# Fewer table transposes, two-tile copies, later stores and a reordered entry in a hybrid decoder block

## The chip, the core and the metric

The kernel runs on one core of one Trainium2 chip. The metric is the device time of an execution in microseconds (us); the time of a kernel is the median of its runs. Engines are called by their short names: PE (TensorE), DVE (VectorE), ACT (ScalarE), POOL (GpSimd) and SP (SyncE, which here only issues DMAs). ACT issues DMAs too, in the same instruction stream as its arithmetic.

## The reference

One decoder layer over 1024 tokens of width 1024, in float32: two SwiGLU feed-forward halves around a merge of two token mixers, with an RMS norm ahead of each part.

```python
def reference(x, ...):                       # x: (1, 1024, 1024)
    h = x + 0.5 * swiglu(rms_norm(h), w1, w3, w2)          # FFN 1, d_ff = 2816
    u = rms_norm(h)
    q, k, v, pz, gate_logits = split(u @ w_in)             # 3 x 768, 512, 2 x 1024 columns
    gates = sigmoid(gate_logits)
    y_attn = dilated_mixture_attention(q, k, v) @ w_branch_attn
    y_pool = multiscale_pool(pz, pool_w, pool_scale) @ w_branch_pool
    h = h + (gates[0] * y_attn + gates[1] * y_pool) @ w_out
    h = h + 0.5 * swiglu(rms_norm(h), w1', w3', w2')       # FFN 2
    return rms_norm(h, final_norm)
```

The attention has 3 groups of 4 heads of 64 dimensions, with windows and dilations (128, 1), (512, 4) and (2048, 16). The first 16 of the 64 dimensions of q and k are rotated by tables of cosines and sines (RoPE). The groups are combined by their softmax denominators.

## The kernel before, in words

**Products.** Every float32 operand is split into a high part, which ACT rounds to the matmul's format, and a low part, the rest, which DVE or POOL subtracts. A product of two operands is three matmuls: high by high, high by low, low by high (`three`). On top of that lies a 2 x 2 block scheme with seven products instead of eight (Strassen in Winograd's form): `Sevens` and `Quad` for the products with stationary weights, `Down` for the down projections. A `Quad` product has 12 matmuls of 128x512 with k-major order, the three terms of one k together; its weight operand (`operand`) is a sum on DVE, a high half on ACT (L304) and a low half on POOL or DVE (L307). Operands are prepared two products ahead.

**Stages, with their times in the profile.** The entry of FFN 1 to 60 us; its up projections to 460; its down projection (`Down.run`, 42 steps of 24 matmuls) to 632; the entry of the mix to 690; the input projection to 1045; attention to 1167; merges and the product with `w_out` to 1262; then FFN 2 in the same three parts, and the final norm to 1916.

**Order.** All of it stands in `tc.manual_schedule()`: every engine runs its instructions in the order in which the program writes them, and waits for the tiles that others write. Moving a call in the source moves its instructions in the queue of each engine that it uses, ahead of or behind whatever the other calls put there.

**What the change touches.**

- `Entry.run` takes the eight tiles of a stage's norm in turn: it scales rows, transposes them on PE into the blocks of X, and keeps high and low halves of the block sums (`Rows` and `Parts`; their `lower` is the DVE subtraction that frees a PSUM bank), with the first products of the stage in between. Its last tile (t = 7) is written out apart.
- `load_rope`, `widen`, `make_table`: the RoPE tables arrive by token. POOL copies them four times over (L1318), PE transposes 24 blocks of 128x128 (L1325), ACT copies the result (L1327) and stores it in DRAM (L1328), one group of heads at a time, as tasks of FFN 1's `Down.run` (steps 9 to 22). `load_table` on SP reads them back later.
- `Mix.rotate` is a generator that the input projection advances by one yield unit a product. For both halves `a` it stores the 16 rotary rows of q or k (L1103, two stores) and the whole rows (L1105, one store) through ACT, then reads the rotary rows back in another order (L1108), also through ACT. The number that it yields is how many products pass before it goes on.
- `Mix.store` stores a block of gates, by SP, and the very last one by ACT (L1094).
- `gather` copies the outputs of one attention slot from PSUM into the group's buffer `own` (L1701), two copies of 64x128 a slot; `values` computes two slots into one bank.
- `merge(k)` multiplies the attention's output by `w_branch_attn` for one block (six matmuls, L1803), times the gate on DVE (L1805), plus the other branch on POOL; `split_o` and `step_o` (L1979, L1991) are the operands and the matmuls with `w_out`.
- `Down.begin` splits the operands of a step: `b`, the weights, then `a`, the left side (L745 on ACT, L749 on DVE or, for some steps' `a`, on POOL).
- `with_gain`, `send_out`, `send_low` close the final norm: squares on ACT (L2171), the gain and scale on DVE (L2167, L2181, L2191) or ACT (L2185), and the output's DMAs.

Of the kernel before, what the change touches and what calls it, by code (L numbers as in the profile page):

```python
# [126 lines left out]
def tile_block(  # L127
# [163 lines left out]
    class Sevens:  # L291


        def __init__(self, name, X, fw, fs=None):
            self.name, self.X, self.fw, self.fs = name, X, fw, fs or fw
            self.n_lo = 0
            self.by_term = False
# [12 lines left out]
        def product(self, p, w, x, start=True):  # L310
            hi, lo = self.X[x]
            order = [(k, q) for k in range(4) for q in range(3)]
            if self.by_term:
                order = [(k, q) for q in (0, 2, 1) for k in range(4)]
            for n, (k, q) in enumerate(order):
                r = slice(k * P, (k + 1) * P)
                a, b = three((w[:, 0, r], w[:, 1, r]), (hi[:, k, :], lo[:, k, :]))[q]
                pe.matmul(p, a, b, start=(start and n == 0), stop=(n == 11), skip_group_check=not start)  # L318
# [66 lines left out]
    class Rows:  # L385


        def __init__(self, X, what, src, t, tag="acc"):
            q = t % 4
            self.hi, self.lo = (v[:, :, q * P:(q + 1) * P] for v in X[what])  # L390
            p = self.flat = bank(tag, f"x_{what}_{t}")
            self.p = p.rearrange("p (k q) -> p k q", k=4)
            for k in range(4):
                pe.transpose(self.p[:, k, :], src[:, k * P:(k + 1) * P], ident)
            ac.activation(self.hi, self.p, AF.Copy)
# [20 lines left out]
    class Entry:  # L416
# [18 lines left out]
        def run(self, high, after, first=0):  # L435
# [84 lines left out]
            after(t)  # L520

# [106 lines left out]
    def up(sv, sums, between, name, room, begun):  # L628
# [3 lines left out]
        with tc.manual_schedule():  # L632
            last = ORDER[-1]
            items = [(q, w, m, out) for q in begun for w, out in ((q.A, q.a_out), (q.B, q.b_out))
                     for m in ORDER if m not in (1, 2)]
            then = Pair(sv, len(begun), sums)
            ahead = [(w, m) for _, w, m, _ in items] + [(then.A, m) for m in ORDER[:2]]
            parts, res = [], []
            for k, (q, w, m, out) in enumerate(items):
                ahead[k + 2][0].operand(ahead[k + 2][1])  # L640
                res.append(w.run(m))
                if m == last:
                    raws.depth = 6 if q is not begun[-1] else 4
                if k > 0:
                    p, _, m, out = items[k - 1]
                    out(m, res[k - 1])
# [58 lines left out]
    class Down:  # L705
# [3 lines left out]
        def __init__(self, name, sums, half_tile, pair):  # L709
# [5 lines left out]
            self.n_lo = 0  # L715
# [17 lines left out]
        def split(self, side, srcs, n):  # L733
# [4 lines left out]
            self.n_lo += 1  # L738
            whole = len(srcs) == 1 and srcs[0].shape[1] > 1
            eng = gp if self.n_lo % 4 == 0 and 1 < n < self.last_shared else ve  # L740
# [27 lines left out]
        def begin(self, i):  # L768
# [3 lines left out]
            w = self.split("b", self.right.pop(i), i)  # L772
# [3 lines left out]
            self.ops[i] = (self.split("a", [self.g.pop(i)], i), w)  # L776
# [99 lines left out]
    def begin_up1():  # L876
# [55 lines left out]
        sv1.by_term = True  # L932
        entry.product(0)
        sv1.by_term = False
# [82 lines left out]
    table_dram = [dram.tile([P, 2, HALF], F32, name=f"table{g}") for g in range(GROUPS)]  # L1017
# [19 lines left out]
    class Mix:  # L1037
# [51 lines left out]
        def store(self):  # L1089
            yield 3  # L1090

            queue = nc.sync if self.q < len(MIX) - 1 else nc.scalar
            for a in range(2):
                queue.dma_start(gate_dram[self.g][:, a], self.y[a])  # L1094

        def rotate(self):
# [4 lines left out]
            for a in range(2):  # L1101
# [4 lines left out]
                yield 1 + 2 * a  # L1106
# [192 lines left out]
    with sbuf("steps1", "right") as pool:  # L1299
# [7 lines left out]
        given, wide = [], {}  # L1307

        def load_rope():
            given.append(own_row("rope")[:, :768].rearrange("p (i c) -> p i c", i=GROUPS * NT))  # L1310
            nc.sync.dma_start(given[0], c_rope)

        def widen(g):
            wide[g] = own_row(f"wide{g}").rearrange("p (s j t a c) -> p s j t a c", s=2, j=4, t=2, a=4)
            for s in range(2):
                for t in range(2):
                    src = given[0][:, g * NT + 4 * t:g * NT + 4 * t + 4, None, 16 * s:16 * s + 16]
                    gp.tensor_copy(wide[g][:, s, :, t], src.to_broadcast([P, 4, 4, 16]))  # L1318

        def make_table(g, tag):  # L1320
            tab = own_row(f"table{g}").rearrange("p (s c) -> p s c", s=2)
            for s in range(2):
                p = bank(tag, f"table{g}_{s}")
                for j in range(4):
                    pe.transpose(p[:, j * P:(j + 1) * P], wide[g][:, s, j].rearrange("p t a c -> p (t a c)"),  # L1325
                                 ident)
                ac.activation(tab[:, s, :], p, AF.Copy)  # L1327
            nc.scalar.dma_start(table_dram[g], tab)  # L1328
# [20 lines left out]
        def scale_in_place(t):  # L1349
# [179 lines left out]
    def by_token(g, d, v):  # L1529
# [6 lines left out]
        return [(by[b], v.rearrange("p (r b) c -> b p r c", b=2)[b]) for b in range(2)]  # L1536
# [69 lines left out]
    def masked(s):  # L1606
# [7 lines left out]
        else:  # L1614
            if i == 0:
                own_stats[hp, g] = att_small.tile([P, NT, 4], F32, name=f"own_stats{hp}_{g}")
            st = own_stats[hp, g][:, i, :]
# [52 lines left out]
    def values(q):  # L1670
        both = bank("acc", f"o{q}")
        for s in (2 * q, 2 * q + 1):
# [12 lines left out]
            d["o"] = p  # L1685
# [3 lines left out]
    own = {}  # L1689

    def gather(s):

        hp, g, i = slots[s]
        p = T.pop(s)["o"]
        t0, step, _ = tokens(g, i)
        cols = slice(t0, t0 + step * (P - 1) + 1, step)
        if i == 0:
            own[hp, g] = sums_o.tile([P, S], F32, tag="o", bufs=HPAIRS * GROUPS, name=f"o{hp}_{g}")
        for a in range(2):
            r = slice(a * HD, (a + 1) * HD)  # L1700
            ve.tensor_copy(own[hp, g][r, cols], p[r, a, :])  # L1701
# [134 lines left out]
    with tc.manual_schedule():  # L1836
        load_branch(1)
        load_ring(uses[1], ring_place(1))
        load_gate(1)
# [4 lines left out]
        for q in range(N // 2):  # L1844
# [13 lines left out]
            if q > 2:  # L1858
                gather(2 * q - 6)
                gather(2 * q - 5)  # L1860
# [30 lines left out]
        gather(2 * q - 6)  # L1891
        gather(2 * q - 5)
# [5 lines left out]
        for s in range(2 * q - 4, 2 * q):  # L1898
            gather(s)
# [123 lines left out]
    with tc.manual_schedule():  # L2023
        for k in range(6):
# [5 lines left out]
            if k > 1:  # L2030
# [4 lines left out]
        for k in range(6, 11):  # L2035
# [121 lines left out]
    def low_half(t):  # L2157
# [4 lines left out]
        if t == 6:  # L2162
# [15 lines left out]
    def send_out(t):  # L2178
# [5 lines left out]
        if t > 5:  # L2184
# [10 lines left out]
    def after2(m, t):  # L2195
# [5 lines left out]
        elif m == len(DOWN) - 1:  # L2201
# [6 lines left out]
            elif t < 3:  # L2208
                send_low(3 + t)
            else:  # L2210
# [98 lines left out]
```

## Time and profile before

| | us |
|---|---|
| median of 3 runs | 1920.96 (1918.78 to 1922.57) |
| the profiled execution | 1918.08 |
| its span in the profile | 1916.3 |

The page gives busy times of the engines over the span. A line of a timeline has the start in us, the duration in us, the engine, the line of the kernel, the operation, what it writes and reads, and the number of instructions drawn together; in brackets stands how long the engine sat idle before it and what released it. ACTq and SPq are the DMA issues in the queues of ACT and SP. The granted TensorE clock of the profiled execution is 0.999 of full speed.

### The profile page before, as it was taken

What the parts mean: (1) busy time and instruction counts of PE and PEld (TensorE: products, weight loads), DVE (VectorE), ACT (ScalarE), POOL (GpSimd) and SP (SyncE); (2) the same over time, 40 slices, a digit from 0 to 9 for tenths busy, and PEclk for the clock granted to TensorE, in tenths of its full rate; (3) what the DMA queues carried; (4) which work ended last, traced back from release to release, by engine and by line L of the source; (5) the groups of instructions that cost most, each with busy time, mean ns of one, the idle gap of its engine ahead of it and who ended that gap; (6) DMA issues with size and microseconds to landing.
All of it is one profiled execution on the core that took longest, in us unless ns stands there. A gap on an engine that the chain in (4) does not pass through costs nothing. (4 is left out here: it accounts for less than half of the span.)

```text
span 1916.3 us, 24859 instructions
## 1 busy us (share of the span) xinstructions
PE 1893.5 (99%) x8840; PEld 1564.1 (82%) x8840; DVE 1341.5 (70%) x2023; ACT 775.3 (40%) x1397; POOL 713.8 (37%) x544
## 2 busy tenths in 40 slices
PE   9999999999999999999999999999999999999998
PEld 7788888888888887888887888887888888888886
DVE  6886556557676776657875897888665556577777
ACT  7333323333345542334445762263333323333344
POOL 4433333331222353535545365643333333322121
PEclk9999999999999999999999999999999999999999
DMA  4155223336465636765578987643433223454664
GB/s 189 55 191 173 83 88 115 127 116 220 150 237 202 200 100 217 246 233 183 203 252 307 283 238 266 248 168 120 172 111 132 83 89 115 149 194 136 200 212 165
DMA packets 147436, 333.56 MB, mean 174 GB/s; under 512 B 20208, under 2 KB 40944, under 8 KB 145776
## 3 DMA queue, kind: packets, MB, share of 16 engines
q1 hardware_dynamic: 138384, 307.74, 47.6%
q10 hardware_dynamic: 8928, 24.23, 3.7%
q8 instruction: 70, 1.15, 0.2%
q14 instruction: 54, 0.44, 0.1%
HBM read 229.61 MB, written 102.30 MB: 173 GB/s over the span
## 5 line engine op out<-in xcount | busy, mean ns | idle before, releaser
L787 PE MATMUL d_f<-bhi_f,ahi_f 128*128 128x512 f32 x616 | 240.5, 390 | 0.5 <-ACT h L402 0.5
L787 PE MATMUL d_f<-bhi_f,alo_f 128*128 128x512 f32 x616 | 240.1, 390 | 0.1
L787 PE MATMUL d_f<-blo_f,ahi_f 128*128 128x512 f32 x616 | 239.7, 389 | 0.0
L318 PE MATMUL u_mixm<-xhi_t_mix,wc_mixm 128*128 128x512 f32 x608 | 195.6, 392 | 1.3 <-POOL wc_mixm L307 0.9
L749 POOL TENSOR_TENSOR alo_f<-g_f,ahi_f 128x512 fp32r<-128x512 f32 x60 | 83.7, 1413 | 271.0 <-ACT ahi_f L745 262.2
L318 PE MATMUL u_mixm<-xhi_b_mix,wc_mixm 128*128 128x512 f32 x456 | 148.6, 392 | 3.0 <-ACT wc_mixm L304 2.8
L787 PEld LDWEIGHTS d_f<-bhi_f,alo_f 128*128 128x128 f32 x616 | 115.6, 188 | 25.3 <-POOL alo_f L749 0.9
L318 PEld LDWEIGHTS u_mixm<-xhi_t_mix,wc_mixm 128*128 128x128 f32 x608 | 113.7, 188 | 27.3 <-POOL wc_mixm L307 3.5
L787 PEld LDWEIGHTS d_f<-bhi_f,ahi_f 128*128 128x128 f32 x616 | 115.6, 188 | 24.7 <-ACT h L402 0.9
L787 PEld LDWEIGHTS d_f<-blo_f,ahi_f 128*128 128x128 f32 x616 | 115.7, 188 | 23.9
L318 PE MATMUL u_mixm<-xlo_t_mix,wc_mixm 128*128 128x512 f32 x304 | 118.4, 389 | 0.0
L307 POOL TENSOR_TENSOR wc_mixm<-s_mixm,wc_mixm 128x512 fp32r<-128x512 f32 x52 | 78.1, 1503 | 101.8 <-ACT wc_mixm L304 87.0
L318 PEld LDWEIGHTS u_mixm<-xhi_b_mix,wc_mixm 128*128 128x128 f32 x456 | 85.6, 188 | 22.3 <-issue 4.0
L304 ACT ACTIVATE wc_mixm<-s_mixm 128x512 fp32r<-128x512 f32 x76 | 47.6, 629 | 109.4 <-DVE s_mixm L360 43.3
L318 PE MATMUL u_mixm<-xlo_b_mix,wc_mixm 128*128 128x512 f32 x228 | 88.8, 390 | 0.0
L745 ACT ACTIVATE ahi_f<-g_f 128x1024 fp32r<-128x1024 f32 x84 | 81.9, 975 | 3.1 <-DMA g_f<-gs_f 3.0
L307 POOL TENSOR_TENSOR wc_mixm<-raw,wc_mixm 128x512 fp32r<-128x512 f32 x40 | 57.8, 1447 | 54.9 <-ACT wc_mixm L304 53.5
L1991 PE MATMUL wo<-w_o,o_hi 128*128 128x512 f32 x224 | 69.2, 390 | 0.0
L745 ACT ACTIVATE bhi_f<-s_f2w 128x512 fp32r<-128x512 f32 x55 | 32.6, 627 | 87.7 <-DVE s_f2w L765 77.3
L318 PEld LDWEIGHTS u_mixm<-xlo_t_mix,wc_mixm 128*128 128x128 f32 x304 | 57.1, 188 | 11.7
L745 ACT ACTIVATE bhi_f<-s_f1w 128x512 fp32r<-128x512 f32 x55 | 33.0, 630 | 78.0 <-DVE s_f1w L765 73.1
L749 DVE TENSOR_TENSOR alo_f<-g_f,ahi_f 128x1024 fp32r<-128x1024 f32 (+1 forms) x48 | 57.6, 1199 | 8.0 <-ACT ahi_f L745 8.0
(1333 smaller groups left out, 5075.9 us busy)
## 6 DMA issues: line engine op xcount, KB each, us to landing
g_f<-gs_f SPq DMA_DIRECT2D x70, 512.0 KB, 4.5
gs_f<-y_f SPq DMA_DIRECT2D x88, 256.0 KB, 2.5
raw<-in_w2a_dram SPq DMA_DIRECT2D x35, 512.0 KB, 4.0
raw<-in_w2b_dram SPq DMA_DIRECT2D x35, 512.0 KB, 3.9
gs_f<-gb_f SPq DMA_DIRECT2D x46, 256.0 KB, 2.3
raw<-in_w1a_dram SPq DMA_DIRECT2D x22, 512.0 KB, 4.7
raw<-in_w3a_dram SPq DMA_DIRECT2D x22, 512.0 KB, 6.0
raw<-in_w1b_dram SPq DMA_DIRECT2D x22, 512.0 KB, 4.4
```

What stands on the lines that cost most here:

```text
L304: ac.activation(w[:, 0], src, AF.Copy)
L307: eng.tensor_tensor(w[:, 1], src, w[:, 0].bitcast(F32), op=OP.subtract)
L318: pe.matmul(p, a, b, start=(start and n == 0), stop=(n == 11), skip_group_check=not start)
L745: ac.activation(hi[:, c], src, AF.Copy)
L749: eng.tensor_tensor(lo[:, d], src[:, o], hi[:, d].bitcast(F32), op=OP.subtract)
L787: pe.matmul(self.banks[m][t], l, r, start=(first and q == 0), stop=(last and q == 2))
L1991: pe.matmul(banks[m][t], l, r, start=(st == 0 and j == 0 and q == 0), stop=(st == 1 and j == 1 and q == 2))
```

## The change

Eight edits in one kernel:

1. The tables are transposed as they arrive, in 6 blocks of 128x128 instead of 24, all as one task of step 10. ACT copies the result twice and stores it with eight DMAs. `load_table` reads each table with two DMAs that repeat it over the heads; POOL's widening goes.
2. In `Entry.run`, for the last tile, the bank of `t3` is taken first but its transposes come after the turned rows and `b22`'s; some `lower` calls change places; and the first product after the entry runs its three terms one after the other, (0, 1, 2), instead of k by k.
3. `rotate` yields `3 - a` instead of `1 + 2 * a` after the stores of half `a`: the second half's stores come two products later, the read-back one product later.
4. The last gate store moves from ACT to SP, behind the first ring loads of the attention.
5. `gather` copies two slots at a time, 64x256. The statistics' layout changes with it.
6. Seven merges instead of six stand ahead of `step_o(0)`.
7. In the final norm, tile 5's gain product comes earlier and its low half is scaled by ACT in `send_out` instead of by DVE in `send_low`.
8. `Down.begin` splits `a` before `b`, and in `up` the output of product 5 is written ahead of the next operand.

```diff
 class Sevens: def product
-            if self.by_term:
-                order = [(k, q) for q in (0, 2, 1) for k in range(4)]
+            if self.terms:
+                order = [(k, q) for q in self.terms for k in range(4)]
+                self.terms = None
...
 class Entry: def run, last tile
             self.product(i)
-            r3 = Rows(X, "t3", t3, t)
+            p3 = bank("acc", f"x_t3_{t}")
             p12 = turned(y, t)
+            s = Rows(X, "b22", y[:, HIGHS], t, "mm")
+            r3 = Rows(X, "t3", t3, t, p=p3)
             r4 = Parts(X, "t4", t2, t - 1)
             self.more(0, 2)
             t2 = bank("acc", f"x_t2_{t}")
             second(r3, t2, t)
             r4.lower()
             r2 = Parts(X, "t2", t2, t)
+            r3.lower()
             self.more(0)
             r2.lower()
             self.product(k)
-            s = Rows(X, "b22", y[:, HIGHS], t)
             self.out(i)
-            r3.lower()
             first_less(p12, t)
...
             self.out(k)
             after(t)
+            self.sv.terms = (0, 1, 2)
...
 def up
+                p, _, before, out = items[k - 1]
+                if before == 5:
+                    out(before, res[k - 1])
                 ahead[k + 2][0].operand(ahead[k + 2][1])
                 res.append(w.run(m))
...
 class Down: def split, def begin
-            eng = gp if self.n_lo % 4 == 0 and 1 < n < self.last_shared else ve
+            eng = gp if side == "a" and n % 2 and 1 < n < self.last_shared else ve
...
-            w = self.split("b", self.right.pop(i), i)
+            a = self.split("a", [self.g.pop(i)], i)
+            self.ops[i] = (a, self.split("b", self.right.pop(i), i))
...
-            self.ops[i] = (self.split("a", [self.g.pop(i)], i), w)
...
 class Mix: def store, def rotate
             yield 3
-            queue = nc.sync if self.q < len(MIX) - 1 else nc.scalar
+            if self.q < len(MIX) - 1:
+                self.send()
+
+        def send(self):
             for a in range(2):
-                queue.dma_start(gate_dram[self.g][:, a], self.y[a])
+                nc.sync.dma_start(gate_dram[self.g][:, a], self.y[a])
...
                 nc.scalar.dma_start(qk_dram[u][a].rearrange("h d c -> (h d) c"), y[a])
-                yield 1 + 2 * a
+                yield 3 - a
...
 def load_table
-        nc.sync.dma_start(tables[g], table_dram[g])
+        for t in range(2):
+            src = table_dram[:, 2 * g + t].rearrange("c s j p -> c (s j p)")
+            dst = tables[g][t * HD:(t + 1) * HD].rearrange("p s c -> p (s c)")
+            nc.sync.dma_start(dst, src[None].to_broadcast([4, 16, 1024]))
...
-        def widen(g): ...
-        def make_table(g, tag): ...
+        def make_tables(tag):
+            tab = own_row("table")[:, :768]
+            for c, n in ((0, 4), (4, 2)):
+                p = bank(tag, f"table_{c}")
+                for j in range(n):
+                    pe.transpose(p[:, j * P:(j + 1) * P], given[0][:, (c + j) * P:(c + j + 1) * P], ident)
+                ac.activation(tab[:, c * P:(c + n) * P], p[:, :n * P], AF.Copy)
+            tab = tab.rearrange("p (b c) -> p b c", c=P)
+            for n in range(8):
+                j, a = divmod(n, 2)
+                nc.scalar.dma_start(table_dram[:, :, a, j], tab[16 * n:16 * n + 16])
...
-            9: [(widen, 0)],
-            10: [(make_table, 0, "mm")],
-            15: [(widen, 1)],
-            16: [(make_table, 1, "acc")],
-            21: [(widen, 2)],
-            22: [(make_table, 2, "mm")],
+            10: [(make_tables, "mm")],
...
 def gather
-        p = T.pop(s)["o"]
-        t0, step, _ = tokens(g, i)
-        cols = slice(t0, t0 + step * (P - 1) + 1, step)
+        p = outs.pop(q).rearrange("p (s a c) -> p s a c", s=2, a=2)
...
-            ve.tensor_copy(own[hp, g][r, cols], p[r, a, :])
+            ve.tensor_copy(o[r], p[r, :, a, :])
...
 attention's start
         load_ring(uses[1], ring_place(1))
+        mixes[-1].send()
         load_gate(1)
...
 attention's loop
-                gather(2 * q - 6)
-                gather(2 * q - 5)
+                gather(q - 3)
...
 merges and w_out
-        for k in range(6):
+        for k in range(7):
             merge(k)
...
-            if k > 1:
+            if 1 < k < 6:
                 reload(k - 2)
         split_o(1)
         step_o(0)
         sum_o(2)
-        for k in range(6, 11):
+        for k in range(7, 11):
...
 final norm
-        if t == 6:
+        if t in (5, 6):
             with_gain(t)
...
-        if t > 5:
+        if t > 4:
             ac.activation(y[:, LOWS], y[:, LOWS], AF.Copy, scale=st[:, 3:4])
             nc.scalar.dma_start(out[rows, LOWS], y[:, LOWS])
...
-            elif t < 3:
-                send_low(3 + t)
-            else:
+            elif t == 1:
+                send_low(4)
+            elif t == 3:
                 send_out(7)
```

More of the change, by code (lines that the diff above doesn't have):

```diff
@@ L644, in up @@
                 if k > 0:
-                    p, _, m, out = items[k - 1]
-                    out(m, res[k - 1])
+                    if before != 5:
+                        out(before, res[k - 1])
                     for g in parts:
@@ L1303, in own_row @@
             return pool.tile([P, D], F32, tag="row", bufs=3, name=n)
-        given, wide = [], {}
+        given = []
         def load_rope():
[L1310 to L1328, printed above, removed]
+            given.append(own_row("rope")[:, :768])
+            nc.sync.dma_start(given[0].rearrange("p (i c) -> p i c", i=GROUPS * NT), c_rope)
+        def make_tables(tag):
[9 more added lines that the diff above has]
+                nc.scalar.dma_start(table_dram[:, :, a, j], tab[16 * n:16 * n + 16])
         def rows_first(t, tag):
@@ L1897, in tile_block @@
         values(q - 1)
-        for s in range(2 * q - 4, 2 * q):
-            gather(s)
+        gather(q - 2)
+        gather(q - 1)
         for n in range(8):
```

38 lines of the change are left out of this document (20 added, 18 removed).

## The prediction

> **What bounds the kernel now.** I read the page's engine shares first, then the waits of TensorE (PE), then the timelines around those waits.
>
> ```profile
> span 1916.3 us, 24859 instructions
> ...
> PE 1893.5 (99%) x8840; PEld 1564.1 (82%) x8840; DVE 1341.5 (70%) x2023; ACT 775.3 (40%) x1397; POOL 713.8 (37%) x544
> ```
> ```profile
> 499.98 0.40 PE L787 MATMUL d_f<-bhi_f,alo_f 128*128 128x512 f32 x1
> 500.21 1.04 PE L1325 MATMUL table<-ident,wide 128*128 128x128 f32 x8
> 501.01 0.47 PE L787 MATMUL d_f<-bhi_f,ahi_f 128*128 128x512 f32 x1
> 501.32 0.39 PE L787 MATMUL d_f<-blo_f,ahi_f 128*128 128x512 f32 x1
> ```
> ```profile
> 1908.24 0.39 PE L787 MATMUL d_f<-bhi_f,alo_f 128*128 128x512 f32 x1
> ```
> PE is busy for 99% of the span, and the matmul stream is dense: from one 128x512 matmul to the next start it takes 0.23 us (499.98 to 500.21; one lasts 0.40, overlapped). The last one starts at 1908.24 of 1916.3, so some 8 us are tail. Only three things can shorten the time: PE instructions taken away, PE gaps closed, tail. These are the gaps, by what ended them:
>
> ```profile
> PE u_mixm L318 <- ACT wc_mixm L304: 2.9, 3, 2.4
> PE wo L1991 <- DVE o_lo L1979: 1.1, 2, 0.7
> ...
> PE s L1603 <- POOL xhi_b_mix L1240: 1.0, 1, 1.0
> PE u_f20a L318 <- DVE xlo_t_f L398: 0.9, 1, 0.9
> PE u_mixm L318 <- POOL wc_mixm L307: 0.9, 2, 0.6
> ...
> PE x_t L394 <- POOL s_f1t L443: 0.7, 1, 0.7
> ...
> PE u_f21a L318 <- DVE y_f L562: 0.5, 1, 0.5
> PE s L1603 <- DVE o L1710: 0.5, 2, 0.3
> ```
> Columns: total us, times, longest. The list is short and no entry passes 3 us, so no part of this change can be worth tens of us. An execution of 1918.08 us had this span of 1916.3 (1.8 around it). It lies 2.9 under the median of 1920.96; I work out differences on the profiled execution and put them on the median. 0.2%, 3.84 us, is about what a measurement of this kernel can tell from no change.
>
> **Table transposes (24 become 6).**
>
> ```profile
> 501.97 0.33 ACTq L1328 DMA_DIRECT2D table<-table  x1
> ```
> Above, eight transposes hold PE from 500.21 to 501.01, 0.80 us, and the matmul after the next comes 0.31 instead of 0.23 later: 0.88 a group, 2.65 for the three groups. One group of six costs about 6 x 0.1 + 0.07 = 0.67. Gain 2.0 on the path itself. The POOL copies that widened the rows go too; no wait names them. The price: eight stores from ScalarE's queue (ACT) in one step, 8 x 0.33 = 2.7 us, in place of one in each of three. Behind them stand the step's own ACT splits, then the POOL subtraction of the left operand, then PE two steps on. A Down step is 24 x 0.23 = 5.5 us, and operands are prepared two steps ahead, so I take the delay as covered. If one of the eight also waits for an earlier load to land, up to 1.5 us could come back. Value -2.0, ends -2.0 and -0.5.
>
> **Rotation stores (second half two items later).** This is the largest gap.
>
> ```profile
> 719.79 4.32 ACTq L1103 DMA_DIRECT2D rot<-y_m  x2
> ...
> 725.11 0.63 ACT L304 ACTIVATE wc_mixm<-s_mixm 128x512 fp32r<-128x512 f32 x1 [4.70 <-DMA rot<-y_m]
> ```
> ```profile
> 717.73 3.01 SPq L67 DMA_DIRECT2D raw<-in_w_qkv_dram  x4
> ```
> ```profile
> 728.89 0.47 PE L318 MATMUL u_mixm<-xhi_b_mix,wc_mixm 128*128 128x512 f32 x1 [2.41 <-ACT wc_mixm L304]
> ```
> ```profile
> 754.91 3.48 ACTq L1103 DMA_DIRECT2D rot<-y_m  x2
> ...
> 760.49 0.63 ACT L304 ACTIVATE wc_mixm<-raw 128x512 fp32r<-128x512 f32 x1 [5.21 <-DMA rot<-y_m]
> ```
> Two stores, 0.8 us elsewhere, take 4.32, and ACT's next weight split starts only after them. In the built program the DMAs of SP and ACT take turns, in program order, on eight completion semaphores, and a store cannot be issued before the DMA eight places ahead of it has landed: here the weight loads that SP issued at 717.73. PE then idles 2.41. The second case, 754.91, holds ACT's next split back to 760.49 and costs PE some 1.3 in three shorter gaps (0.6 of them the longest in the POOL row above). The stores of the second half now come two products of 12 matmuls later, 2 x 12 x 0.23 = 5.5 us.
>
> ```profile
> raw<-in_w_qkv_dram SPq DMA_DIRECT2D x24, 256.0 KB, 4.5
> ```
> ```profile
> rot<-y_m ACTq DMA_DIRECT2D x24, 64.0 KB, 4.1
> ```
> By then loads that take 4.5 us have landed, so both blocks should go: 2.4 + 1.3 = 3.7. What is late next is the read-back of the stored rows, also on ACT: it now follows the second half's stores by two products instead of three, 5.5 us against a landing of 4.1, and one of six may wait a little: 0.2. Value -3.5, ends -4.0 and -1.0 (blocks of like length reappear elsewhere).
>
> **Last gate store from ACT to SP.**
>
> ```profile
> 1047.09 0.81 ACTq L1094 DMA_DIRECT2D gate<-y_m  x2
> ```
> ```profile
> 1047.93 1.28 ACT L1440 ACT_TABLE_LOAD   x1 [0.87 <-ACT y_m L1082]
> ```
> ```profile
> 1045.00:1100.00 55.00, 53.35 (x403) 44.62 (x403) 42.31 (x160) 38.43 (x127) 15.22 (x13) 1.00 0.99 301
> 1100.00:1125.00 25.00, 24.88 (x183) 20.99 (x184) 22.75 (x87) 19.64 (x69) 15.55 (x14) 1.00 0.88 246
> 1125.00:1167.00 42.00, 40.97 (x297) 35.14 (x296) 37.60 (x121) 23.26 (x73) 17.70 (x18) 1.00 0.78 211
> ```
> The table load and the first exponents, for which PE's first transposes wait, start 0.84 earlier. PE idles 55 - 53.35 = 1.65 in the first stretch: 1.0 is the POOL row of xhi_b_mix, set by a split that stays, and the remainder is this. Value -0.8 out of the 0.84, since the transposes follow the exponents one for one; ends -0.9 and 0.
>
> **Gather: two tiles at a copy.**
>
> ```profile
> L1701 DVE COPY o<-o x96: 275/387/415, 1058.4 to 1162.0; 64x128 f32<-64x128 f32 x96
> ```
> ```profile
> 1909.62 0.68 DVE L792 SCALAR_TENSOR_TENSOR h_last<-d_f,h_last 128x512 f32<-128x512 f32 x1
> ```
> From 275 ns for 128 columns and 680 for 512, a column costs 405 / 384 = 1.05 and an instruction 140 ns, as an estimate. 48 copies fewer save VectorE (DVE) 48 x 0.14 = 6.7 us. [...] PE idles 0.12 + 1.03 after 1100, where DVE is busy 37.60 of 42; start to start I read up to 1.9 there. Copies come sooner, banks too, but the other DVE work in front of PE stays. Value -0.8, ends -1.9 and 0.
>
> **Seven merges before the first W_o step.**
>
> ```profile
> 1175.38 0.61 PE L1991 MATMUL wo<-w_o,o_hi 128*128 128x512 f32 x2
> 1176.41 0.50 PE L1991 MATMUL wo<-w_o,o_lo 128*128 128x512 f32 x1 [0.41 <-DVE o_lo L1979]
> 1176.74 0.63 PE L1991 MATMUL wo<-w_o,o_hi 128*128 128x512 f32 x2
> 1178.10 0.50 PE L1991 MATMUL wo<-w_o,o_lo 128*128 128x512 f32 x1 [0.73 <-DVE o_lo L1979]
> ```
> ```profile
> 1174.65 3.38 DVE L1979 TENSOR_TENSOR o_lo<-merged,o_hi 128x512 fp32r<-128x512 f32 x2
> ```
> Start to start PE loses 1176.41 - 1175.61 - 0.23 = 0.57 and 1178.10 - 1176.97 - 0.23 = 0.90. A merge is 6 x 0.23 = 1.4 of matmuls that need nothing from o_lo; moved ahead it fills these gaps, and the lower halves, ahead of it on DVE, come no later. Its own product on DVE then stands in front of the next operand, due a step later. Value -1.3, ends -1.4 and 0 (if the merge's input, which DVE already awaited once from a DMA, is what comes late).
>
> **Entries, Down's splits, tail.** The entry gaps are those of x_t 0.7, u_f20a 0.9, two of POOL's weight low halves 0.3 each, and 0.5 of the ACT row: 2.7. The reorder frees each: transposes no longer wait on the sum, and with terms (0, 1, 2) the weight's low half is asked for at the ninth matmul instead of the third. But behind them stands one chain, seen in the groups:
>
> ```profile
> L307 POOL TENSOR_TENSOR wc_mixm<-s_mixm,wc_mixm 128x512 fp32r<-128x512 f32 x52 | 78.1, 1503 | 101.8 <-ACT wc_mixm L304 87.0
> ```
> DVE's weight sum, queued behind three more low halves, then ACT's split (0.63), then 1.50 on POOL for the next product, which again asks at its third matmul. Counting it through gives -0.6 in the first entry, +0.15 in the mix, about 0 in the third. Value -0.35, ends -2.7 and +0.6. Then Down:
>
> ```profile
> 1901.24 0.68 DVE L749 TENSOR_TENSOR alo_f<-g_f,ahi_f 128x512 fp32r<-128x512 f32 x1
> ```
> Splitting `a` ahead of `b` in Down takes one such DVE operation off the last step's path, where PE slips about 0.35: -0.35, ends -0.4 and 0. The earlier `out` may shave the u_f21a wait: -0.1, ends -0.5 and 0. In the tail:
>
> ```profile
> 1908.96 0.75 DVE L2191 SCALAR_TENSOR_TENSOR n<-h_last,nst_last,gain_final 128x512 f32<-128x512 f32 x1
> ```
> the last accumulation on DVE (1909.62, above) queues behind L2191, which moves to ACT as a scaling of like length plus a DMA issue of 0.34; that delays the last square on ACT in turn. I take -0.4, ends -0.65 and +0.3.
>
> Sum: -2.0 - 3.5 - 0.8 - 0.8 - 1.3 - 0.35 - 0.35 - 0.1 - 0.4 = -9.6. The profiled 1918.08 would be 1908.5; the median, **1911.4**. All favourable ends together give -14.5 (1906.5), all unfavourable ones -0.6 (1920.4).
>
> **Rivals.** *Every gap closes*: the entries' chain has more slack than I counted and DVE's relief closes the attention gaps; about -13.5, 1907.5. For it: several small waits are under 0.5. Against: POOL's 1503 ns stays.
>
> *The stalls only move*: semaphores are still shared, so ACT blocks at other stores (-1.0 there), attention and merges are then held by their DMA loads (DMA share 0.99 before 1100) and give 0; -2.0 - 1.0 - 0.4 = -3.4, 1917.6, no change to be told. That is also the case in which the change does not do what it says: later stores, larger copies, the same PE time.
>
> *Slower, by the read-back*: the six read-backs on ACT wait for stores issued 5.5 us earlier. If these land late, each blocks ACT as the 4.32 block did, and PE loses 2.41 six times: +14.5 - 9.6 = +4.9, 1925.9. It decides where a landing passes 5.5 plus the 4.70 - 2.41 = 2.3 of ACT slack that the same block shows, 7.8 us. Against it: the 4.1 row.
>
> ```profile
> DMA to landing us min/median/max: 1.9/4.5/11.4
> ```
> For it: of all these transfers some take up to 11.4. [...]
>
> **How the numbers follow.** Forecast 0.54, every gap closes 0.20, stalls move 0.17, read-back 0.09. Faster by over 0.2% are the first two, 0.74; within 0.2% the third, 0.17; slower 0.09. The range runs from below the all-closed case, 1905.5, to 1920.0, which takes in the moved stalls and nearly all unfavourable ends; the read-back is left out.
>
> **What the changed profile would show.** One group of six transposes near 500 us with the matmul stream unbroken for the two steps after it (else the eight stores bite); no `rot` in TensorE's or ACT's waits between 715 and 765 (else stalls moved); wo's waits on o_lo down to about 0.2; copies of 64x256 at roughly 0.41 to 0.65 us; the last matmul at about 1899. New long ACT queue entries at the read-back would make the prediction wrong, as would a PE idle sum above 12 us ahead of the last matmul (15 now).

## The result

The changed kernel takes 1938.11 us (median of 4, 1935.84 to 1940.20), the kernel before 1920.88. The ratio is 1.0090, 95% interval 1.0073 to 1.0107: 17 us slower, where 9.6 us faster was forecast. The range ended at 1920.0.

The profiled execution took 1937.50 us. From its page, first the span and the engines, then two of the costliest groups of instructions (busy us, mean ns, then the idle time ahead of them and who ended it):

```profile
span 1935.7 us, 24801 instructions
...
PE 1899.1 (98%) x8822; PEld 1567.2 (81%) x8822; DVE 1335.8 (69%) x1975; ACT 775.4 (40%) x1394; POOL 722.3 (37%) x532
...
L752 POOL TENSOR_TENSOR alo_f<-g_f,ahi_f 128x512 fp32r<-128x512 f32 x60 | 95.2, 1603 | 268.4 <-ACT ahi_f L748 268.4
...
L748 ACT ACTIVATE ahi_f<-g_f 128x1024 fp32r<-128x1024 f32 x84 | 82.7, 984 | 91.8 <-DMA g_f<-gs_f 42.9
```

PE has 18 instructions less and is busy 5.6 us longer. Idle PE grew from 22.8 to 36.6 us. Two rows of Down stand out: POOL's subtraction of `a` went from 1413 to 1603 ns, and ACT, which sat idle 3.1 us ahead of the split of `a`, now sits idle 91.8.

PE's waits in the changed kernel:

```profile
PE u_mixm L319 <- DVE y_m L1071: 6.6, 3, 5.3
PE d_f L790 <- ACT h L403: 4.6, 1, 4.6
PE d_f L790 <- DVE blo_f L752: 2.9, 6, 0.7
PE d_f L790 <- ACT bhi_f L748: 2.9, 1, 2.9
PE u_mixm L319 <- ACT wc_mixm L304: 1.5, 1, 1.5
```

Down (`d_f`) waited 0.5 us before; it now waits over 10. The mix (`u_mixm`) has one gap of 5.3 us. That gap costs more than its length. The same stretch of the changed kernel (columns: us; busy us and matmuls of PE; PEld, DVE, ACT, POOL; granted clock; DMA share; GB/s), and matmuls after it from its timeline:

```profile
771.00:774.00 3.00, 0.92 (x5) 0.42 (x3) 0.00 (x0) 0.00 (x0) 0.00 (x0) 1.00 0.31 112
774.00:777.00 3.00, 0.00 (x0) 0.00 (x0) 1.25 (x3) 1.15 (x2) 0.68 (x1) 0.77 0.61 174
777.00:780.00 3.00, 2.81 (x7) 2.26 (x8) 2.97 (x5) 0.63 (x1) 0.90 (x2) 0.50 1.05 334
780.00:783.00 3.00, 3.00 (x10) 2.33 (x9) 0.40 (x2) 0.83 (x2) 1.53 (x2) 0.59 1.05 322
```
```profile
777.76 0.63 PE L319 MATMUL u_mixm<-xlo_b_mix,wc_mixm 128*128 128x512 f32 x1
778.19 1.05 PE L319 MATMUL u_mixm<-xhi_b_mix,wc_mixm 128*128 128x512 f32 x2
```

After 5.3 us of idle PE the granted clock is 0.50, and matmuls start 0.43 us apart instead of 0.23, up to 782.5: twelve of them, some 2.5 us on top. The kernel before had a gap of 2.41 us and no slow matmul behind it. The length of a gap alone does not decide it, though. A gap of 2.92 us at 1895 in the changed kernel is followed by 0.50 as well, and behind one of 2.20 us at 729 in a later run the mean from 729 to 732 is 0.58. The stretch behind it in the kernel before (gap of 2.41 us) and in that run (f1_a_even, gap of 2.20 us):

```profile
729.00:732.00 3.00, 3.00 (x14) 2.48 (x15) 2.97 (x4) 0.72 (x2) 3.00 (x3) 1.00 0.34 131
```
```profile
729.00:732.00 3.00, 2.98 (x8) 2.37 (x9) 2.97 (x3) 0.84 (x3) 2.91 (x3) 0.58 0.34 131
```

### The profile page after: what moved, and what is told of

Read it like the earlier page. It is cut to its first block, busy times and chain, and to the rows that moved or that the text cites. A ratio compares the mean times of both kernels' runs of the same rounds, so it can differ in the third digit from the quotient of the medians.

```text
span 1935.7 us, 24801 instructions
## 1 busy us (share of the span) xinstructions
PE 1899.1 (98%) x8822; PEld 1567.2 (81%) x8822; DVE 1335.8 (69%) x1975; ACT 775.4 (40%) x1394; POOL 722.3 (37%) x532
## 4 chain that ended last, share of the span: by engine, by line
PE 35%; DMA 5%; DVE 4%; issue 2%; ACT 2%; POOL 1%; SPq 1%; ACTq 0%; POOLq 0%; DVEq 0%
PE d_f L790 6%; PE wo L1992 3%; PE u_mixm L319 1%; PE ya L1805 1%; PE u_f20b L319 1%; PE u_f21a L319 1%; PE u_f210a L319 1%; PE u_f29b L319 1%; PE u_f29a L319 1%; PE u_f28b L319 1%; PE u_f28a L319 1%; PE u_f27b L319 1%; PE u_f27a L319 1%; PE u_f26b L319 1%; PE u_f26a L319 1%
## 5 line engine op out<-in xcount | busy, mean ns | idle before, releaser
L752 POOL TENSOR_TENSOR alo_f<-g_f,ahi_f 128x512 fp32r<-128x512 f32 x60 | 95.2, 1603 | 268.4 <-ACT ahi_f L748 268.4
L748 ACT ACTIVATE ahi_f<-g_f 128x1024 fp32r<-128x1024 f32 x84 | 82.7, 984 | 91.8 <-DMA g_f<-gs_f 42.9
```

The costliest lines, as they stand in the source:

```text
L748: ac.activation(hi[:, c], src, AF.Copy)
L752: eng.tensor_tensor(lo[:, d], src[:, o], hi[:, d].bitcast(F32), op=OP.subtract)
```

## The experiments

Ratios to the kernel before, each with its 95% interval:

| kernel | what it is | ratio |
|---|---|---|
| after | the whole change | 1.0090 [1.0073, 1.0107] |
| e1_b_first | after, `b` split first | 1.0044 [1.0027, 1.0061] |
| e2_table_rows | after, tables loaded whole | 1.0104 [1.0087, 1.0121] |
| e6_three | after, `b` first, whole loads, stores spread | 1.0013 [1.0004, 1.0023] |
| e7_rotate_old | e6 with rotate's old yields | 0.9981 [0.9969, 0.9993] |
| f4_sp_stores | e6 with rotate's stores by SP | 0.9965 [0.9954, 0.9977] |
| e3_a_first_alone | before, `a` first | 1.0078 [1.0058, 1.0099] |
| f1_a_even | before, `a` first in even steps | 1.0001 [0.9987, 1.0015] |
| f2_a_odd | before, `a` first in odd steps | 1.0086 [1.0070, 1.0102] |
| g4_a_first_dve | before, `a` first, POOL not used | 1.0009 [1.0000, 1.0019] |
| e4_tables_alone | before, the table edit | 1.0063 [1.0048, 1.0079] |
| g1_tables_whole | e4, tables loaded whole | 1.0007 [0.9998, 1.0016] |
| g2_tables_spread | e4, stores spread | 1.0047 [1.0032, 1.0062] |
| e5_rotate_alone | before, rotate's new yields | 1.0013 [1.0003, 1.0022] |
| g3_before_sp | before, rotate's stores by SP | 0.9978 [0.9968, 0.9988] |
| f3_extra_dma | before, one more DMA | 1.0006 [0.9995, 1.0016] |
| e8_rest | before, the remaining edits | 0.9984 [0.9974, 0.9995] |
| h1_rest_sp | e8 with rotate's stores by SP | 0.9948 [0.9936, 0.9961] |
| h2_all_sp_old | f4 with rotate's old yields | 0.9952 [0.9938, 0.9965] |

**The order of a and b in Down.** First undone in the changed kernel, then done alone. (In e3, f1 and f2 the line that chooses the engine is the changed kernel's, so that POOL keeps the same share: the low halves of `a` in odd steps.)

```diff
 e1_b_first, on after (e3_a_first_alone is the reverse, on before)
-            a = self.split("a", [self.g.pop(i)], i)
-            self.ops[i] = (a, self.split("b", self.right.pop(i), i))
+            w = self.split("b", self.right.pop(i), i)
...
+            self.ops[i] = (self.split("a", [self.g.pop(i)], i), w)
```

> The changed kernel with one edit undone: Down.begin splits b (the weights) before a again. Theory (a before b costs): in the changed profile PE's gaps that hang on Down's operands are 0.3 to 0.6 us each at 528 to 567, about 5.7 at 630 to 635 and 4.5 near 1895, and each of the two long ones is followed by some ten matmuls 0.43 us apart instead of 0.23 (1.5 and 2.8 us). Undone, all of that goes but 0.9 that was there before: 1938.1 - 15.3 = about 1923, and no matmul 0.43 us apart after 620 us except in the mix. Rival (the stalls come from the table stores and loads, which shift the completion semaphores, and the order of a and b only shows it): 1936 to 1938, the gaps near 630 and 1895 stay.

> The kernel before with one edit: Down.begin splits a before b. Theory (a before b costs): long PE gaps near 630 and near the end of FFN 2's down projection, 1920.9 + 13 to 16 = 1934 to 1937. Rival (it needs the other edits): 1919 to 1922.

Alone it costs 0.78%, 15 us; undone it gives back 0.46%, 9 us, where I expected 15. By the medians it is the largest single loss, but its interval overlaps that of the tables' 0.63% below. The changed kernel at one of its odd steps:

```profile
632.62 2.96 POOL L752 TENSOR_TENSOR alo_f<-g_f,ahi_f 128x512 fp32r<-128x512 f32 x2 [2.50 <-ACT ahi_f L748]
633.04 3.09 DVE L752 TENSOR_TENSOR blo_f<-s_f1w,bhi_f 128x512 fp32r<-128x512 f32 x2 [0.94 <-ACT bhi_f L748]
...
637.96 1.20 ACT L403 ACTIVATE h<-x_b 128x512 f32<-128x512 f32 x2 [3.46 <-DVE xlo_b_mix L399]
```

Two subtractions of 0.69 us each take 3.09 on DVE while POOL subtracts beside them. Behind them stand the mix's first low halves, then ACT's L403, which frees a PSUM bank for which PE waits 4.6 us. At another step ACT waits 8.1 us for `g` and holds up `b`:

```profile
1893.38 1.06 ACT L748 ACTIVATE ahi_f<-g_f 128x1024 fp32r<-128x1024 f32 x1 [8.10 <-DMA g_f<-gs_f]
1894.35 1.14 ACT L748 ACTIVATE bhi_f<-s_f2w 128x512 fp32r<-128x512 f32 x2
```

Which of the two costs: POOL works in odd steps only.

```diff
 f1_a_even: par = 0; f2_a_odd: par = 1, on before
+            if i % 2 == par:
+                a = self.split("a", [self.g.pop(i)], i)
+                w = self.split("b", self.right.pop(i), i)
+            else:
+                w = self.split("b", self.right.pop(i), i)
+                a = None
 g4_a_first_dve, on before with a first
-            eng = gp if side == "a" and n % 2 and 1 < n < self.last_shared else ve
+            eng = ve
```

> The kernel before with a split ahead of b in the even steps of Down only, where DVE subtracts a's low half. Theory (ACT's high half of a waits for the load of g, and b's, behind it, waits too: ACT's 8.1 us wait at 1893 in the changed kernel stood in such a step): the stall near 1895 comes, the one near 630 does not: + 6 to 8 on 1918.2. Rival (POOL's subtraction of a now runs beside DVE's of b and slows both): no loss here.

> The kernel before with a split ahead of b in the odd steps only, where POOL subtracts a's low half in all but the first and last steps. Theory of the shared work (POOL beside DVE: in the changed kernel two subtractions of b took 3.06 us at 508 and 3.09 at 633 instead of 1.29): the stall near 630 comes, the one near 1895 does not: +6 to 9 on 1918.2. Rival (all of it is the load of g that ACT waits for): both stalls stay in part, or none.

> The kernel before with a split ahead of b in every step and all low halves on DVE, none on POOL. Theory (POOL beside DVE is the cost): no stall near 630 and 1895 by slowed subtractions, although DVE has 60 x 0.7 us more to do: 0.999 to 1.003. Rival (ACT's order of a and b is the cost): the loss of 1.0078 stays.

The even steps cost nothing, the odd ones all of it, and without POOL's work the order of ACT is worth 0.09%. So what costs is POOL's subtraction beside DVE's. In the groups of 440 to 640 us, of the kernel with even steps turned:

```profile
L747 DVE TENSOR_TENSOR blo_f<-s_f1w,bhi_f 128x512 fp32r<-128x512 f32 x52 | 33.7, 685 | 8.9 <-ACT bhi_f L743 8.9
L747 POOL TENSOR_TENSOR alo_f<-g_f,ahi_f 128x512 fp32r<-128x512 f32 x30 | 41.4, 1397 | 135.9 <-ACT ahi_f L743 135.9
```

and of the kernel with odd steps turned:

```profile
L747 DVE TENSOR_TENSOR blo_f<-s_f1w,bhi_f 128x512 fp32r<-128x512 f32 x48 | 39.3, 850 | 12.9 <-ACT bhi_f L743 12.6
L747 POOL TENSOR_TENSOR alo_f<-g_f,ahi_f 128x512 fp32r<-128x512 f32 x30 | 49.3, 1661 | 130.2 <-ACT ahi_f L743 130.2
```

850 against 685 ns on DVE, 1661 against 1397 on POOL. My expectation for the even steps was wrong: the wait for `g` did not bring its stall there. With the odd ones alone turned, the stall near 1895 is there: PE stands idle 3.3 us, against 3.7 with all steps turned and 0.6 with the even ones. The trace shows a link. A product of the final norm on DVE (L267) meets POOL's subtraction too; SP stores its result, and the load of `g` stands behind that store in SP's queue. In the changed kernel, where POOL's started first, at 1885.02, and below it in the run with even steps turned, where POOL's starts second, at 1876.59, and is the slow one with 2.11 us:

```profile
1885.09 2.30 DVE L267 SCALAR_TENSOR_TENSOR hn_n<-h_last,nst,gain_final 128x1024 f32<-128x1024 f32 x1 [0.66 <-POOL nst L264]
1887.42 0.34 SPq L2199 DMA_DIRECT2D out_dram<-hn_n  x1
1887.86 1.21 SPq L735 DMA_DIRECT2D g_f<-gs_f  x2
```
```profile
1876.26 1.28 DVE L267 SCALAR_TENSOR_TENSOR hn_n<-h_last,nst,gain_final 128x1024 f32<-128x1024 f32 x1 [0.66 <-POOL nst L264]
```

With 2.30 instead of 1.28 us the load of `g` goes out 1.0 us later. Whether that is the whole of this stall was not tried.

**The tables.** The edit alone, then with one half mended at a time:

```diff
 e2_table_rows on after, g1_tables_whole on e4
+        def repeat(b):
+            src = table_dram[:, b].rearrange("c s j p -> c (s j p)")
+            nc.sync.dma_start(wide_dram[b].rearrange("b c x -> c b x"), src[:, None].to_broadcast([16, 4, 1024]))
...
+        nc.sync.dma_start(tables[g].rearrange("p s c -> p (s c)"),
+                          wide_dram[2 * g:2 * g + 2].rearrange("t b c x -> (t b c) x"))
 g2_tables_spread on e4
+            **{11 + n: [(store_table, n)] for n in range(8)},
```

> The kernel before with the table edit alone (6 transposes, eight stores in step 10, two repeating loads a table). By the prediction's term -2.0, 1919. By the changed profile: -2.0 for the transposes, +1.7 for two gaps near 510 behind the eight stores (5.2 us of ACT's queue), and +3 to +7 in the mix if the loads on 4 DMA engines make its stall: 1923 to 1928. Rival (rotate makes the mix stall): 1920 to 1921.

> The kernel before with the table edit, but each table loaded as one block over all 16 DMA engines, its repeats written out in DRAM by six DMAs of FFN 1's down projection. The table edit as it stands cost 12 (1.0063). Theory (the loads on 4 engines hold back the weights behind them): the gaps of 4.1 and 5.0 at 761 to 772 shrink to the 1 to 4 of the kernel before, -5 to -8 against the edit as it stands: 1.002 to 1.0035 of the kernel before, the stores' gaps near 510 stay. Rival (the stores are it): 1.005 or more.

> The kernel before with the table edit, but its eight stores go one to a step. Theory: the gaps of 2.1 near 510 go, those in the mix stay or move: -2 to -3 against the edit as it stands, 1.0045 to 1.0055. Rival (the stores are the larger half): 1.002 or less.

> The changed kernel with another table load: after the eight stores, six DMAs on SP in steps 22 to 27 of FFN 1's down projection write the four repeats out in DRAM, rows outermost, and each table then comes by one DMA of 128 contiguous rows, as in the kernel before. Theory (the repeating loads, whose slowest dimension is 4, run on 4 of 16 DMA engines, and stores behind them land late): ACT's 6.1 us wait at 769 to 775 and PE's 5.3 us gap at 777 go, with the slow matmuls behind it: -5 to -8, 1930 to 1933. Rival (the stores' new place in rotate makes the stall, through the shared semaphores): the stall stays, 1937 to 1939.

Alone the table edit costs 0.63%, 12 us, more than the 4 to 9 that I expected. Whole loads take 0.56 of it away. Spread stores take 0.16, which lies within the noise of the two intervals; the gaps near 510, shown below, are gone in that run. With the edit alone, these loads are issued at 746; the stretch behind them, and the loads of weights issued with them (KB each, us to landing):

```profile
748.00:752.00 4.00, 4.00 (x21) 3.32 (x20) 3.53 (x5) 2.75 (x6) 2.45 (x2) 1.00 0.57 105
```
```profile
raw<-in_w_qkv_dram SPq DMA_DIRECT2D x2, 256.0 KB, 13.0
```

and the same with whole loads:

```profile
748.00:752.00 4.00, 4.00 (x21) 3.32 (x20) 3.30 (x5) 2.72 (x6) 2.45 (x2) 1.00 0.88 263
```
```profile
raw<-in_w_qkv_dram SPq DMA_DIRECT2D x2, 256.0 KB, 4.4
```

105 GB/s against 263, and weights that land after 13.0 us instead of 4.4: the repeating load, of `[4, 16, 1024]`, uses few of the 16 DMA engines. In the changed kernel's trace, from 760.1 to 760.9, when only its table loads were moving, packets took 25.3% of the 16 engines' time, that of four. With the edit alone the DMA share right behind the issue, from 747 to 750, is 0.20, against 0.71 with whole loads. That the weights wait for these engines is the author's estimate from the two landings; no run shows it by itself. In the changed kernel the DMA share falls to 0.31 in the stretch at 771 shown above, where stores of `v`, issued behind the table loads, land after 11.4 us.

The eight stores:

```profile
501.13 5.21 ACTq L1330 DMA_DIRECT2D table<-table  x8
506.39 1.06 ACT L748 ACTIVATE ahi_f<-g_f 128x1024 fp32r<-128x1024 f32 x1 [5.29 <-DMA table<-table]
```
```profile
509.43 0.50 PE L790 MATMUL d_f<-blo_f,ahi_f 128*128 128x512 f32 x1 [0.61 <-DVE blo_f L752]
511.12 0.50 PE L790 MATMUL d_f<-blo_f,ahi_f 128*128 128x512 f32 x1 [0.72 <-DVE blo_f L752]
```

Each takes ACT's queue 0.65 us to issue, where the old store took 0.33; ACT is idle 5.29 us and two gaps follow.

In the changed kernel whole loads alone gained nothing (e2). Its gap in the mix was still 4.5 us, since rotate's stores held ACT there, and the gaps in Down grew: from 440 to 640 us PE's waits on `blo_f` went from 2.3 to 4.2. The six copies in DRAM stand among these gaps, at 567 to 593; whether they cause them was not tried. The losses hide one another: alone they sum to 0.78 + 0.63 + 0.13 - 0.16 = 1.38%, together they are 0.90%.

**Rotate.** The yields alone, and taken back out of the mended kernel:

```diff
 e5_rotate_alone, on before (e7_rotate_old is the reverse, on e6)
-                yield 1 + 2 * a
+                yield 3 - a
 e6_three, on after, with e1's order of the splits and e2's whole loads
-            for n in range(8):
+        def store_table(n):
...
+            **{11 + n: [(store_table, n)] for n in range(8)},
+            **{22 + b: [(repeat, b)] for b in range(6)},
```

> The kernel before with one edit: rotate yields 3 - a, the second half's stores two products later. By the prediction's term -3.5: 1915.4 against a kernel before of 1918.9. Theory now (a store waits for whichever DMA stands eight places ahead on the shared semaphores, so a new place only changes which one): ACT is again held for 4 to 7 us once or twice between 715 and 790, PE's gaps there sum to between 3 and 9 instead of 3.9: 1918 to 1924. Rival (the prediction's mechanism is right and only the tables spoil it): 1915 to 1916.5.

> The changed kernel with three things mended: b is split before a; the eight table stores go one to a step, in steps 11 to 18; and the repeats are written out in DRAM so that a table is one load over all 16 DMA engines. If tables and the order of a and b were all: 1938.1 less 15 for a and b, 2 for the stores: about 1917 to 1920 on a kernel before of 1918.9, with a remaining stall near 775 worth some 5. If the stores' issue were not what makes the gaps at 509: about 1923.

> The run above (b first, stores spread, whole loads) with rotate's old yields 1 + 2 * a. If the new place of the stores makes the stall near 775 to 781 (theory: rotate), -3 to -6 against that run. If the shifted turn of the semaphores makes it (theory: turns), no gain, or a stall at another place: within 2 of that run.

They cost 0.13%, 2.5 us, alone instead of gaining 3.5, and 0.32% within the mended kernel. Later stores are held as long as early ones were, only elsewhere. From ACT's timeline with the new yields alone, then of the changed kernel:

```profile
764.31 0.34 ACTq L1105 DMA_DIRECT2D qk<-y_m  x1
764.75 0.63 ACT L304 ACTIVATE wc_mixm<-raw 128x512 fp32r<-128x512 f32 x1 [4.24 <-DMA raw<-in_w_qkv_dram]
```
```profile
765.23 0.63 ACT L304 ACTIVATE wc_mixm<-s_mixm 128x512 fp32r<-128x512 f32 x1 [4.49 <-DMA table_in<-table]
768.40 0.63 ACT L304 ACTIVATE wc_mixm<-s_mixm 128x512 fp32r<-128x512 f32 x1 [1.53 <-DVE s_mixm L370]
772.92 1.06 ACTq L1107 DMA_DIRECT2D rot<-y_m  x2
774.60 0.40 ACTq L1109 DMA_DIRECT2D qk<-y_m  x1
775.09 0.63 ACT L304 ACTIVATE wc_mixm<-raw 128x512 fp32r<-128x512 f32 x1 [6.06 <-DMA rot<-y_m]
```

With the yields alone, ACT's wait behind the store at 764.31 lasts 4.24 us and ends with a load of weights that lands. In the changed kernel the DMA ahead on the semaphore is first a table load (4.49 us), then a store of `v` issued behind the table loads, which lands at 772.90, 0.02 us ahead of the store at 772.92. So the two edits meet in one stall.

If ACT standing still is the loss, the stores should go to an engine that does nothing else:

```diff
 g3_before_sp on before, f4_sp_stores on e6
-                    nc.scalar.dma_start(given[:, a, n].rearrange("t r c -> r t c"),
+                    nc.sync.dma_start(given[:, a, n].rearrange("t r c -> r t c"),
...
-                nc.scalar.dma_start(qk_dram[u][a].rearrange("h d c -> (h d) c"), y[a])
+                nc.sync.dma_start(qk_dram[u][a].rearrange("h d c -> (h d) c"), y[a])
```

> The run with b first, stores spread and whole loads (1.0013 of the kernel before), with rotate's three stores a half issued by SP instead of ACT, in the changed kernel's new places. Theory (the loss is ACT standing still in its own instruction stream while a store waits): no wait of ACT on rot between 715 and 790, the 4.7 us gap near 766 with its slow matmuls gone, -5 to -7: 1913 to 1915. Rival (SP is now held and the weights come late): the gap turns into a wait on raw loads, 1918 to 1924.

> The kernel before with rotate's three stores a half issued by SP instead of ACT, at the old places. This is the block that the prediction wanted to remove by later stores. Theory (ACT standing still while a store waits is the loss): the gaps at 729 and 761 go: -2.5 to -4, 0.998 to 0.9987. Rival (SP holds the weights instead): 0.9995 to 1.003.

Both gain: 0.22% on the kernel before, 0.48% on the mended one. From 690 to 800 us, f4_sp_stores leaves PE idle 0.7 us of 110, where the kernel before had 3.8:

```profile
690.00:800.00 110.00, 109.31 (x497) 89.89 (x496) 70.31 (x99) 34.97 (x62) 45.44 (x36) 1.00 0.68 221
```

Does the turn of the semaphores matter by itself? One load more, used by nothing, early in the kernel before:

```diff
 f3_extra_dma, on before
+            28: [(lambda: nc.sync.dma_start(own_row("extra")[:, :768].rearrange("p (i c) -> p i c", i=GROUPS * NT),
+                                            c_rope),)],
```

> The kernel before with one more DMA on SP, a second load of the small RoPE input in step 28 of FFN 1's down projection, that nothing uses. It moves every later DMA on by one place in the turn of eight semaphores and does no more. Theory (which DMA a store waits for is a matter of its turn): PE's two gaps at 729 (2.6) and 761 (1.35) change, one of them by over 1 us, and the time by 1 to 5 either way. Rival (the turn does not matter, only how the queues are loaded): both gaps as before within 0.3, time within 1.5.

The median is that of the kernel before, against the 1 to 5 us that I expected. In the profiled execution PE's gap at 730 was 2.8 us instead of 2.4, and those at 765 to 767 summed to 2.0 instead of 0.8, both with slow matmuls behind them. But that execution took 1925.37 us, the longest of ten. So the shift moves single waits; that it changes the time is not shown.

**What is left, and a better kernel.** The changed kernel with the three losing parts taken back (the old tables, the old yields, `b` first), then with rotate's stores by SP; and f4_sp_stores with the old yields:

```diff
 e8_rest, on after
-            a = self.split("a", [self.g.pop(i)], i)
-            self.ops[i] = (a, self.split("b", self.right.pop(i), i))
+            w = self.split("b", self.right.pop(i), i)
...
+            self.ops[i] = (self.split("a", [self.g.pop(i)], i), w)
...
-            10: [(make_tables, "mm")],
+            10: [(make_table, 0, "mm")],
...
 e8_rest on after, and h2_all_sp_old on f4_sp_stores
-                yield 3 - a
+                yield 1 + 2 * a
 h1_rest_sp, on e8_rest
-                    nc.scalar.dma_start(given[:, a, n].rearrange("t r c -> r t c"),
+                    nc.sync.dma_start(given[:, a, n].rearrange("t r c -> r t c"),
```

> The changed kernel without the table edit, without rotate's yields and with b split first: what is left is the entries' order, the gate store, the gather, the seven merges, the tail and up. The prediction's terms for these sum to -0.35 - 0.8 - 0.8 - 1.3 - 0.4 - 0.1 = -3.75: 1915 on a kernel before of 1918.9. If the later DMAs only move the attention's waits (rival): 1917 to 1919.

> The kernel before with the edits that gained (entries' order, gate store, gather, seven merges, tail, up: 0.9984 alone) and rotate's stores issued by SP at the old places (0.9978 alone); tables as before, b first. If the two add up: 0.9962, 1912.7 on a kernel before of 1920. Rival (they fill the same gaps): 0.9975.

> The run with b first, table stores spread, whole table loads and rotate's stores by SP (0.9965), with rotate's old yields. Against h1_rest_sp it has the 6 transposes instead of 24, worth 2.0 on PE by the prediction's count. If that gain survives: 0.9952, 1910.8. If the eight stores and six copies in DRAM eat it: 0.996 to 0.997. If the new yields matter once SP issues the stores: it differs from 0.9965 by over 0.002.

The remaining edits gain 0.16%, 3.1 us. With rotate's stores on SP they gain 0.52% (1913.06 against 1921.80), with the tables and Down's order as before: the fastest found, level with h2. The 6 transposes in place of 24 add nothing to it that can be seen (0.9952 against 0.9948). In the profiled executions PE stands idle 1.6 us near 1896 with them and 0.5 near 1894 without; near 1060 it is 1.3 us in both, but with them the granted clock is 0.79 from 1055 to 1063, and without them 1.00. Whether the table stores or copies cause this was not tried.

## Why the prediction was wrong, point by point

- **Down's order: the step that failed most.** It was priced at -0.35 from its last step alone, where DVE subtracts both sides. It applies to 84 steps, and in the odd ones it starts POOL's subtraction together with DVE's. The price is +15 us. The profile before has the sign of it: the slowest of DVE's subtractions (min/median/max ns) ran at 459.12, beside one of POOL's from 458.61 to 460.35.

```profile
L749 DVE TENSOR_TENSOR blo_f<-s_f1w,bhi_f x55: 677/691/1777, 438.9 to 650.3; 128x512 fp32r<-128x512 f32 x55
```

- **Tables: the load had no price at all.** The term held the transposes (0.67 forecast, 499.59 to 500.16 and 0.08 more measured: right) and the issue of the stores (0.33 each forecast, 0.65 measured), whose delay was taken as covered; two gaps of 0.6 and 0.7 us followed. The two loads that replace one were not weighed; they cost about 10.8 of the 12 us, by the run with whole loads.
- **Rotate: the mechanism was right, the remedy was not.** ACT does stand still while a store waits its turn, and PE does lose that; g3 removes it and gains 4.2 us, close to the 3.7 counted. The trace of the kernel before has the 839 DMA issues of SP and ACT on eight semaphores, 104 or 105 on each; the store that was held to 723.80 went out 0.02 us after the load issued at 717.73, the one ahead of it on its semaphore, had landed. But a later place meets other DMAs ahead on the semaphore: in the changed kernel a table load, which landed at 764.82, and a store of `v`, which landed at 772.90. The rival "the stalls only move" named that, with 0.17 and a price of 2.5; the read-back, the slower rival, held ACT in the changed kernel once for 2.7 us, up to 781.8, and no gap of PE followed.
- **Length of a gap.** All gaps were counted at their length. Behind its gaps of 4.6, 5.3 and 2.9 us PE came back at half clock, which the prediction had no term for; by the starts of the matmuls, 0.43 us apart instead of 0.23, the three stalls cost some 7 us more.
- **Right in sum, the rest (-3.75 forecast, -3.1 measured, with an interval of -5.0 to -1.0).** Its terms were not run one by one. The merges' waits on `o_lo` L1979 went. The table load of the exponents starts right behind the last gate, at 1063.12 behind 1063.10. The tail from the last matmul's start fell from 8.06 to 7.10, over twice the forecast of 0.4:

```profile
1928.60 0.39 PE L790 MATMUL d_f<-bhi_f,alo_f 128*128 128x512 f32 x1
```

- **Gather: size right, worth wrong.** Copies of 64x256 take 409 to 651 ns, as worked out, and DVE is busy 5.7 us less over the span. PE's two waits on DVE `o` L1710, 0.5 us together, stay at 0.5 with the remaining edits: DVE's work ahead of PE was other work. The tail gave more than forecast and the gather nothing that can be seen, so the sum of the rest is right in part by luck.

```profile
L1703 DVE COPY o<-o x48: 409/620/651, 1073.6 to 1177.9; 64x256 f32<-64x256 f32 x48
```

## What to carry to other kernels

Ahead of any change of order on one engine, ask which two engines it makes work at the same time, not only which waits it shortens: a subtraction on GpSimd beside one on VectorE took 1.2 times as long on both, on average (1661 ns against 1397, and 850 against 685), and here that was the largest loss. Look at how many DMA engines a rewritten DMA keeps busy: here a load that repeats its source four times, outermost, had four of 16 at work, and with it came 105 GB/s instead of 263 and weights, queued behind it, that landed 8.6 us later. An engine that computes on the critical path should not issue stores that may wait; moving their issue to an idle engine gained 0.22% where moving them in time lost 0.13%.

## What the runs showed of the hardware that was not expected

Two DVE subtractions of 128x512, 1.29 us alone, took 3.09 beside POOL's. A store of 16 partitions with six rows of 512 B each took ACT's queue 0.65 us to issue, against 0.33 for one of 128 rows. After 5.3 us without a matmul the granted clock was 0.50, for some 5 us; after 2.41 us it was still 1.00 in one run, and after 2.20 us it was 0.58 in another, as the mean from 729 to 732.
